# Moving a layer's weight-sum transfers in the schedule, and adding the residual by accumulating stores

## The chip, the core and the metric

The kernel runs on one core of a Trainium2 chip. The metric is the device time of one execution in microseconds (us). TensorE (PE in the profile) multiplies, VectorE (DVE) and ScalarE (ACT) do elementwise work, GpSimd (POOL) does some elementwise work and issues a few transfers, and SyncE (SP) issues nearly all transfers.

## What is computed

One decoder layer on 512 tokens of width 2048, all in float32. Cut to what matters here:

```
h = rms_norm(x, norm_w) * (1 + scale) + shift        # scale, shift, gate from silu(c) @ w_ada
proj = h @ w_in                                      # 2048 x 21056
y_a = (sliding-window attention * silu gate) @ w_o_swa
y_b = (gated delta rule over 16 key / 32 value heads, normed, gated) @ w_o_dn
y = sigmoid(mg_a) * y_a + sigmoid(mg_b) * y_b
return x + gate * (y @ w_out)
```

## The kernel before

**Products.** Every projection is made from tiles of 128 output channels by 512 tokens. `channel_tile` (L244) loops over 16 blocks of 128 input channels, and `mm3` (L237) makes each block's product of three 128x512 matmuls (L240 to L242), because each float32 operand is kept as a high and a low part in a matmul format. So one tile is 48 matmuls. Its weights are one transfer of 1 MB on SP's queue (`load_job`, L200, tile `raw`), and each half of it (24 matmuls) is split into `whi` by a cast on ACT (L52) and `wlo` by a subtraction on DVE (L53). There are two `raw` buffers and three of each split half. A half that is not split in time stops PE.

**Stages.** A startup makes h while `w_ada` (32 MB) streams in. The key stretch follows: 31 tiles (12 key heads, 16 merge gates of one branch, 3 of the other), and beside them the generators of 16 key heads (`keys`, L679) with their convolution (`conv`, L572), transposes, decay matrices `E` and stores, and a triangular solve on DVE (`solve`, L767) in two halves. Then 16 rounds of `heads` (L816), each with five tiles (q, v, v, z, z) and a generator `queries` (L846) and `scan` (L926) that carries the delta rule; then branch B, attention, and `finish` (L1299), where the output product runs on seven products in place of eight and so needs sums of blocks of `w_out`.

**What sets the order.** `channel_tile` calls `pump` (L81) after every second block, eight times a tile, and each call moves the live generators on. A scheduler then puts all instructions in order, each engine's in a fixed one, by its own estimate of when each can start; each engine runs its list in order and waits where an operand is missing. `behind` (L105) adds an order without a semaphore: what is made inside stands after the last matmul so far. Instructions without it may be put earlier in the lists, as early as their data allow.

**The weight sums.** `weight_sums` (L657) makes 16 sums of 1 MB in DRAM (tiles `wsm`): for each a plain copy from DRAM to DRAM on SP's queue (L671), then a transfer on POOL's queue that adds a second block to it (L675). Some copies read an earlier sum, so SP waits at them until that accumulating transfer has landed. `heads` registers this generator as a side queue at 0.15 steps a pump (L643), without `behind`. `finish` reads the sums as `raww` (L1371).

**The output.** `columns` (L1401) multiplies a 128x512 result by the gate on DVE (L1404), loads the matching piece of x on SP's queue (L1406), adds it on POOL (L1407) and stores the sum on SP's queue (L1408), 16 times.

Of the kernel before, what the change touches and what calls it, by code (L numbers as in the profile page):

```python
# [7 lines left out]
F32 = mybir.dt.float32  # L8
# [3 lines left out]
ALU = mybir.AluOpType  # L12
# [4 lines left out]
P = 128  # L17
T = 512
D = 2048
KT = D // P  # L20
NTB = T // P
# [15 lines left out]
class Layer:  # L37
# [552 lines left out]
    def deltanet(self):  # L590
        tc, nc, a = self.tc, self.nc, self.a
        dram = self.dram
        self.lt_d = dram.tile([2, 2, 16, 4, HD, HD], F32, name="lt_d")
        self.lab_d = dram.tile([VH, HD, 4, HD], F32, name="lab_d")
        self.ta_d = dram.tile([2, 16, 4, HD, HD], F32, name="ta_d")
        self.ts_d = dram.tile([2, 2, 16, 4, HD, HD], F32, name="ts_d")
        self.kT_d = dram.tile([KH, P, T], F32, name="kT_d")
        self.k_d = dram.tile([KH, P, T], F32, name="k_d")
        self.o_d = dram.tile([VH, P, T], F32, name="o_d")
        self.ws_d = {k: dram.tile([P, 2048], F32, name=f"ws{k[0]}{k[1]}{k[2]}") for k in self.sum_keys()}  # L600
        with ExitStack() as ps:
            self.pmm = ps.enter_context(tc.tile_pool(name="pmm", bufs=2, space=PSUM, reuse_waits="tile"))
            self.ptp = ps.enter_context(tc.tile_pool(name="ptp", bufs=2, space=PSUM, reuse_waits="tile"))
            self.gwk = ps.enter_context(tc.tile_pool(name="gwk", bufs=1, reuse_waits="tile"))
            sol1 = ps.enter_context(tc.tile_pool(name="sol1", bufs=1, side="right", reuse_waits="tile"))
            with ExitStack() as sa:
                wk = sa.enter_context(tc.tile_pool(name="dnA", bufs=2, reuse_waits="tile"))
                sol0 = sa.enter_context(tc.tile_pool(name="sol0", bufs=1, reuse_waits="tile"))
                gp = sa.enter_context(tc.tile_pool(name="gates", bufs=1, reuse_waits="tile"))
                self.go(self.gates(gp), 1)  # L610
                self.keys_done, self.solve_in = [], {}
                self.keep_order = True
                for g in range(NST):
                    self.go(self.keys(wk, g, self.acc_k[g]), 10 + 8 * g)
                for j in range(NFIRST):
                    self.merge_gate("mb", j, self.mb_d)
                self.go(self.solve_load(sol0, 0), 1)
                self.go(self.solve_load(sol1, 1), 1)
                s0 = self.paced(self.solve(sol0, 0, nc.vector), 0.82)
                s1 = self.paced(self.solve(sol1, 1, nc.vector), 0.0)  # L620
                for kind, j in self.mixed():
                    if kind == "k":
                        self.go(self.keys(wk, j, self.channel_tile(f"k{j}")), 0)
                    else:
                        self.merge_gate("mb", j, self.mb_d)
                        if j == KT - 3:
                            s0[1] = 1.2
                for j in range(3):
                    self.merge_gate("ma", j, self.ma_d)
                    if s0 not in self.slow:  # L630
                        s1[1] = 1.1
                self.drain_live()
                self.drain_slow(s0)
                self.keep_order = False
                s1[1] = 0.6
            with ExitStack() as sb:
                wk = sb.enter_context(tc.tile_pool(name="dnB", bufs=2, reuse_waits="tile"))
                self.tt = []
                for n in range(4):
                    t = wk.tile([P, NTB, P], F32, tag=f"tt{n}", name=f"tt{n}", bufs=1)  # L640
                    nc.gpsimd.memset(t[HD:P, :, 0:HD], 0.0)
                    self.tt.append(t)
                self.beside(self.weight_sums(), 0.15, "ws")  # L643
                for g in range(KH):
                    if g == 8:
                        self.drain_slow(s1)
                    self.heads(wk, g)
                for j in range(3, 5):
                    self.merge_gate("ma", j, self.ma_d)
                self.drain_live()  # L650
                self.drain("ws")
        self.dump("o", self.o_d)

    def sum_keys(self):
        return [(s, n, i) for s in ("m7", "m5", "m6", "m4") for n in range(2) for i in range(2)]

    def weight_sums(self):  # L657

        nc = self.nc
        for n in range(2):  # L660
            for i in range(2):
                w = lambda c, r: self.a["w_out"][2 * c + n, 2 * r + i]
                m7, m5, m6, m4 = (self.ws_d[s, n, i] for s in ("m7", "m5", "m6", "m4"))
                steps = [
                    [(m7, w(1, 0), w(1, 1)), (m5, w(0, 0), w(1, 0))],
                    [(m6, m7, w(0, 0))],
                    [(m4, m6, w(0, 1))],
                ]
                for parts in steps:
                    for dst, src, _ in parts:  # L670
                        nc.sync.dma_start(out=dst, in_=src)  # L671
                    for _ in range(2):
                        yield
                    for dst, _, more in parts:
                        nc.gpsimd.dma_start(out=dst, in_=more, accum_op=ALU.add, max_dma_last_dim=8192)  # L675
                    for _ in range(2):
                        yield
# [697 lines left out]
    def output(self, es, wk, A):  # L1375

        tc, nc, a = self.tc, self.nc, self.a
# [23 lines left out]
        def columns(n, c, t, src, sign):  # L1401

            csl = slice(c * 1024 + n * T, c * 1024 + n * T + T)
            nc.vector.scalar_tensor_tensor(out=src, in0=src, scalar=sign, in1=gt[:, c, :], op0=ALU.mult, op1=ALU.mult)  # L1404
            x = wk.tile([P, T], F32, tag="yb", name="x")
            nc.sync.dma_start(out=x, in_=a["x"][t * P : (t + 1) * P, csl])  # L1406
            nc.gpsimd.tensor_tensor(out=src, in0=src, in1=x, op=ALU.add)  # L1407
            nc.sync.dma_start(out=self.out[t * P : (t + 1) * P, csl], in_=src)  # L1408

        def evict(n, name):  # L1410
            TT = nc.vector.tensor_tensor
            for t in range(2):
                b = ps[name, t]
                if name == "m1":
                    o = t * 1024 + n * T
                    nc.sync.dma_start(out=gt[:, t, :], in_=self.gate_d[o : o + T].partition_broadcast(P))
                if name in ("m1", "m5"):
                    k = wk.tile([P, T], F32, tag=f"{name}{t}", name=name, bufs=1)
                    nc.scalar.copy(out=k, in_=b)
                    keep[name, t] = k  # L1420
                elif name == "m2":
                    c = wk.tile([P, T], F32, tag="m", name="c11")
                    TT(out=c, in0=b, in1=keep["m1", t], op=ALU.add)
                    columns(n, 0, t, c, 1.0)
                elif name == "m6":
                    u1, u5 = keep["m1", t], keep["m5", t]
                    u = wk.tile([P, T], F32, tag="m", name="u2")
                    TT(out=u, in0=b, in1=u1, op=ALU.add)
                    TT(out=u1, in0=ps["m7", t], in1=u, op=ALU.add)
                    c = wk.tile([P, T], F32, tag="m", name="c22")  # L1430
                    TT(out=c, in0=u1, in1=u5, op=ALU.add)
                    TT(out=u5, in0=u, in1=u5, op=ALU.add)
                    columns(n, 1, 2 + t, c, 1.0)
                elif name == "m4":
                    k = keep["m1", t]
                    TT(out=k, in0=b, in1=k, op=ALU.subtract)
                    columns(n, 0, 2 + t, k, 1.0)
                elif name == "m3":
                    k = keep["m5", t]
                    TT(out=k, in0=b, in1=k, op=ALU.add)  # L1440
                    columns(n, 1, t, k, -1.0)
# [3 lines left out]
        for i, (n, m, p) in enumerate(items):  # L1445
            name, s, _ = order[m]
# [128 lines left out]
```

## Time and profile before

| what | value |
|---|---|
| runs | 2982.72, 2983.65, 2976.06 us; median 2982.72 |
| profiled execution | 2981.72 us, span 2980.0 us |
| PE busy over the span | 2887.5 us (97%) |
| DVE, ACT, POOL busy | 59%, 36%, 8% |
| moved by the transfer queues | 497.26 MB, mean 167 GB/s |
| of it on POOL's queue (software_dynamic) | 16.78 MB in 2304 packets |
| landing of a 1 MB accumulating transfer | 8.7 / 12.4 / 16.0 us (min, median, max) |

The span is the time from the first to the last recorded instruction; 1.72 us of the profiled execution lie outside it. A busy PE counts overlapping matmuls once. The granted clock is the share of TensorE's full clock in a stretch. A wait is put down to what arrived last.

### The profile page before, as it was taken

Reading aid. Unit: us, or ns where it says so; the run is one execution under the profiler, and the core shown is the slowest. Engines: PE = TensorE matmul, PEld = TensorE weight load, DVE = VectorE, ACT = ScalarE, POOL = GpSimd, SP = SyncE. Lnnn points to the kernel's source line nnn. Section 1 sums busy time; section 2 is a strip of 40 time slices with the busy share of each in tenths; the row PEclk is TensorE's granted clock in tenths of the full one; section 3 lists DMA queues with packets and bytes.
Section 4 is the critical chain, followed back from the end, with each engine's and each line's share of the span. In section 5 each row is a group of like instructions: output and inputs, shape, how many; then the busy total and the mean of one; then the engine's idle time right before and its main releaser. Section 6 shows DMA issues by size and latency. Waiting matters only on the chain. (4 is left out here: it accounts for less than half of the span.)

```text
span 2980.0 us, 38116 instructions
## 1 busy us (share of the span) xinstructions
PE 2887.5 (97%) x14556; PEld 2362.6 (79%) x14556; DVE 1743.3 (59%) x2883; ACT 1087.4 (36%) x2113; POOL 240.3 (8%) x220
## 2 busy tenths in 40 slices
PE   8878989999999999999999999999999999999989
PEld 6666777888888888888888878888788788788867
DVE  7745769777777544455555453433656656554485
ACT  4334423333333433333333322311244344342343
POOL 0013112011100100000100000000100000000012
PEclk9998999999999999999999999999999999999999
DMA  9898695643333533334332475554322222375575
GB/s 387 308 277 245 201 260 167 196 149 122 112 124 122 150 121 107 125 113 133 115 125 95 168 284 203 185 172 163 110 87 87 77 100 101 109 255 172 180 263 204
DMA packets 179592, 497.26 MB, mean 167 GB/s; under 512 B 73137, under 2 KB 75697, under 8 KB 139601
## 3 DMA queue, kind: packets, MB, share of 16 engines
q1 hardware_dynamic: 177106, 478.06, 47.3%
q0 software_dynamic: 2304, 16.78, 2.9%
q8 instruction: 114, 1.87, 0.3%
q14 instruction: 68, 0.56, 0.1%
HBM read 433.09 MB, written 93.00 MB: 177 GB/s over the span
## 5 line engine op out<-in xcount | busy, mean ns | idle before, releaser
L240 PE MATMUL mm<-hh,whi 128*128 128x512 f32 x2784 | 1137.3, 409 | 9.9 <-ACT whi L52 9.2
L242 PE MATMUL mm<-hh,wlo 128*128 128x512 f32 x2784 | 1094.6, 393 | 0.6 <-DVE wlo L53 0.5
L241 PE MATMUL mm<-hl,whi 128*128 128x512 f32 x2784 | 1091.9, 392 | 0.0
L53 DVE TENSOR_TENSOR wlo<-raw,whi 128x1024 fp32r<-128x1024 f32 (+1 forms) x428 | 523.8, 1227 | 522.6 <-ACT whi L52 518.3
L52 ACT CAST whi<-raw 128x1024 fp32r<-128x1024 f32 (+1 forms) x428 | 445.1, 1043 | 940.7 <-PE mm L241 904.0
L240 PEld LDWEIGHTS mm<-hh,whi 128*128 128x128 f32 x2784 | 527.2, 189 | 120.9 <-ACT whi L52 10.3
L242 PEld LDWEIGHTS mm<-hh,wlo 128*128 128x128 f32 x2784 | 525.7, 189 | 116.9 <-DVE wlo L53 2.5
L241 PEld LDWEIGHTS mm<-hl,whi 128*128 128x128 f32 x2784 | 527.5, 189 | 99.9 <-issue 0.8
L240 PE MATMUL mm<-oh,whi 128*128 128x512 f32 x512 | 200.3, 393 | 1.1 <-ACT whi L52 0.9
L242 PE MATMUL mm<-oh,wlo 128*128 128x512 f32 x512 | 199.4, 390 | 0.5 <-DVE wlo L53 0.5
L241 PE MATMUL mm<-ol,whi 128*128 128x512 f32 x512 | 199.5, 390 | 0.0
L893 POOL TENSOR_TENSOR qe<-qe,yq 128x512 f32<-128x512 f32 x32 | 50.5, 1596 | 902.3 <-DMA qe<-eg_rows 850.7
L240 PEld LDWEIGHTS mm<-oh,whi 128*128 128x128 f32 x512 | 96.1, 188 | 22.9 <-ACT whi L52 1.3
L241 PEld LDWEIGHTS mm<-ol,whi 128*128 128x128 f32 x512 | 96.1, 188 | 21.4 <-issue 1.0
L242 PEld LDWEIGHTS mm<-oh,wlo 128*128 128x128 f32 x512 | 96.1, 188 | 21.1 <-DVE wlo L53 1.2
L792 DVE TENSOR_TENSOR A<-A,atmp 128x62 f32<-128x62 f32 (+30 forms) x124 | 111.0, 895 | 1.5
L785 DVE TENSOR_TENSOR atmp<-A 128x62 f32<-128x62 f32 (+30 forms) x124 | 109.0, 879 | 1.4
L742 POOL TENSOR_TENSOR E<-E,neg_g 128x512 f32<-128x512 f32 x64 | 75.4, 1183 | 260.2 <-DMA E<-g_rows 146.5
L53 DVE TENSOR_TENSOR wlo<-raww,whi 128x1024 fp32r<-128x1024 f32 x56 | 70.8, 1268 | 26.2 <-ACT whi L52 24.7
L52 ACT CAST whi<-raww 128x1024 fp32r<-128x1024 f32 x56 | 58.8, 1052 | 59.7 <-PE m L242 46.1
L939 DVE SCALAR_TENSOR_TENSOR r<-pp,neg_eg,vt 128x128 f32<-128x128 f32 x96 | 29.2, 346 | 78.8 <-PE pp L936 77.6
L1260 ACT ACTIVATE sm<-sm,mx,rs 128x256 f32<-128x256 f32 (+1 forms) x128 | 71.7, 561 | 3.3 <-DVE mx L1255 3.3
(326 smaller groups left out, 3154.2 us busy)
## 6 DMA issues: line engine op xcount, KB each, us to landing
raw<-in_w_ch SPq DMA_DIRECT2D x158, 1024.0 KB
wa<-in_w_ada_ss SPq DMA_DIRECT2D x32, 1024.0 KB
raw<-in_w_od SPq DMA_DIRECT2D x32, 1024.0 KB
wsm<-in_w_out POOLq DMA_DIRECT2D x16, 1024.0 KB, 12.4
E<-g_rows SPq DMA_DIRECT2D x64, 256.0 KB
gw<-in_w_ada_gate SPq DMA_DIRECT2D x16, 1024.0 KB
raw<-in_w_os SPq DMA_DIRECT2D x16, 1024.0 KB
raww<-wsm SPq DMA_DIRECT2D x16, 1024.0 KB
```

The source lines that it names most:

```text
L52: self.nc.scalar.copy(out=hi, in_=src)
L53: self.nc.vector.tensor_tensor(out=lo, in0=src, in1=hi.bitcast(F32), op=ALU.subtract)
L240: nc.tensor.matmul(ps, lhsT=wh, rhs=xh, start=first, stop=False)
L241: nc.tensor.matmul(ps, lhsT=wh, rhs=xl, start=False, stop=False)
L242: self.last_mm = nc.tensor.matmul(ps, lhsT=wl, rhs=xh, start=False, stop=last).ins
L742: nc.gpsimd.tensor_tensor(out=E, in0=E, in1=ng, op=ALU.add)
L785: eng.tensor_tensor(out=t, in0=A[:, m : m + 1, m + 1 :].to_broadcast([P, m, n]), in1=A[:, :m, m : m + 1].to_broadcast([P, m, n]), op=ALU.mult,
L792: eng.tensor_tensor(out=A[:, :m, m + 1 :], in0=A[:, :m, m + 1 :], in1=t, op=ALU.add)
L893: nc.gpsimd.tensor_tensor(out=qf, in0=qf, in1=q, op=ALU.mult)
L939: nc.vector.scalar_tensor_tensor(out=r[:, e, :], in0=pp[:, e, :], scalar=self.neg_eg[:, c, 2 * g + e : 2 * g + e + 1], in1=v[e][:, c, :], ...
L1260: nc.scalar.activation(t, t, AF.Exp, scale=r[:, h : h + 1], bias=mx[:, h : h + 1], accum_out=den[:, h : h + 1])
```

## The change

The generator of the weight sums is wrapped so that each of its steps is made inside `behind`. It first copies x into the output, four transfers of 1 MB. `columns` no longer loads x, adds it and stores, but lets POOL's queue add the gated result to the output in DRAM.

```
-                self.beside(self.weight_sums(), 0.15, "ws")
+                self.beside(self.ordered(self.weight_sums()), 0.15, "ws")
...
+    def ordered(self, gen):
+
+        for _ in range(1000):
+            with self.behind():
+                if next(gen, self) is self:
+                    return
+            yield
+
     def weight_sums(self):
 
         nc = self.nc
+        for t in range(NTB):
+            s = slice(t * P, (t + 1) * P)
+            nc.sync.dma_start(out=self.out[s], in_=self.a["x"][s])
+            yield
...
-            x = wk.tile([P, T], F32, tag="yb", name="x")
-            nc.sync.dma_start(out=x, in_=a["x"][t * P : (t + 1) * P, csl])
-            nc.gpsimd.tensor_tensor(out=src, in0=src, in1=x, op=ALU.add)
-            nc.sync.dma_start(out=self.out[t * P : (t + 1) * P, csl], in_=src)
+            nc.gpsimd.dma_start(out=self.out[t * P : (t + 1) * P, csl], in_=src, accum_op=ALU.add)
```

In the lists of the changed kernel the same line of code stands 12 lines further on (9 in `columns`). Three places show how the lists move.

SP's queue at the start of the key stretch, before: `mb_d` is a merge gate's store, `g_rows` and `eg_rows` are the decay rows that the key heads read, `wsm` are the weight sums.

```order
L671 DMA wsm_1142<-in_w_out 16x16384
L266 DMA mb_d<-mth 128x512
L671 DMA wsm_1153<-wsm_1149 16x16384
L568 DMA g_rows<-rows 32x512
L568 DMA eg_rows<-rows 32x512
L200 DMA raw<-in_w_ch 128x2048
```

The same place in the changed kernel:

```order
L266 DMA mb_d<-mth 128x512
L568 DMA g_rows<-rows 32x512
L568 DMA eg_rows<-rows 32x512
L568 DMA b_rows<-rows 32x512
L200 DMA raw<-in_w_ch 128x2048
```

All 32 transfers of the sums have left the key stretch on SP and on POOL. The four copies of x stand among the first round's loads of `heads`, and the sums are spread over the rounds behind it.

ACT's list in the first round of `heads`, before: `yv` and `th` belong to the convolution of a value tile, `zh` and `zth` to a gate tile, `whi` are the split weights that PE waits for.

```order
L576 ACTIVATE yv<-mm,convh 128x512
L730 ACTIVATE junk,ss<-ptq 128x128
L52 CAST whi<-raw 128x1024
L730 ACTIVATE junk,ss<-ptq 128x128
L887 ACTIVATE E<-E 128x512
L730 ACTIVATE junk,ss<-ptq 128x128
L585 ACTIVATE th<-yv 128x512
L52 CAST whi<-raw 128x1024
L843 COPY vt<-ptv 128x512
L52 CAST whi<-raw 128x1024
L576 ACTIVATE yv<-mm,convh 128x512
```

The same place in the changed kernel:

```order
L576 ACTIVATE yv<-mm,convh 128x512
L742 ACTIVATE junk,ss<-ptq 128x128 x2
L585 ACTIVATE th<-yv 128x512
L855 COPY vt<-ptv 128x512
L576 ACTIVATE yv<-mm,convh 128x512
L585 ACTIVATE th<-yv 128x512
L52 CAST whi<-raw 128x1024 x2
L899 ACTIVATE E<-E 128x512 x2
L840 ACTIVATE zh<-mm,dnwh 128x512
L842 ACTIVATE zth<-mm 128x512
L52 CAST whi<-raw 128x1024 x2
```

Of the three casts that stood between the two `yv` none is left there: two follow the second `yv` and its `th`, and the next two follow `zh` and `zth`, which read the gate tile that PE has then finished.

DVE's list at the end of the first round's scan, before: `S`, `r` belong to the scan, `yq` to the next round's query convolution, `A` and `atmp` to the second triangular solve, `ms` begins the output norm.

```order
L976 SCALAR_TENSOR_TENSOR S<-S,egl,pd 128x128 x2
L53 TENSOR_TENSOR wlo<-raw,whi 128x1024
L580 SCALAR_TENSOR_TENSOR yq<-mm,convh,yq 128x511
L792 TENSOR_TENSOR A<-A,atmp 128x17x46
L580 SCALAR_TENSOR_TENSOR yq<-mm,convh,yq 128x510
L939 SCALAR_TENSOR_TENSOR r<-pp,neg_eg,vt 128x128 x2
L580 SCALAR_TENSOR_TENSOR yq<-mm,convh,yq 128x509
L587 SCALAR_TENSOR_TENSOR yq<-th,yq 128x512
L785 TENSOR_TENSOR atmp<-A 128x810
L53 TENSOR_TENSOR wlo<-raw,whi 128x1024
L792 TENSOR_TENSOR A<-A,atmp 128x18x45
L989 SCALAR_TENSOR_TENSOR ms<-osq,epsq 128x4 x2
```

The changed kernel has there no split at all:

```order
L988 SCALAR_TENSOR_TENSOR S<-S,egl,pd 128x128 x2
L580 SCALAR_TENSOR_TENSOR yq<-mm,convh,yq 128x511
L951 SCALAR_TENSOR_TENSOR r<-pp,neg_eg,vt 128x128 x2
L580 SCALAR_TENSOR_TENSOR yq<-mm,convh,yq 128x510
L580 SCALAR_TENSOR_TENSOR yq<-mm,convh,yq 128x509
L587 SCALAR_TENSOR_TENSOR yq<-th,yq 128x512
L1001 SCALAR_TENSOR_TENSOR ms<-osq,epsq 128x4 x2
```

and after ten small rows of the reciprocal root (L59 to L64) it goes on with the norm (`osb`), the gating of the transposed output (`zh`) and only then the splits:

```order
L873 TENSOR_SCALAR epsq<-ss 128x4
L1008 TENSOR_TENSOR osb<-osb,roy 128x512 x2
L1015 TENSOR_TENSOR zh<-pto,zh 128x512 x2
L53 TENSOR_TENSOR wlo<-raw,whi 128x1024 x2
L804 TENSOR_TENSOR A<-A,atmp 128x17x46
```

PE's list of the changed kernel at that place, where `pp`, `pv`, `po` are the scan's last chunk, `ptq` the next round's query transposes and `pto` the output transposes:

```order
L977 MATMUL po<-vn,E 128x128
L948 MATMUL pp<-S,kT 128x256
L958 MATMUL pv<-r,tt_4601 128x128
L976 MATMUL po<-S,qe 128x128
L958 MATMUL pv<-r,tt_4603 128x128
L977 MATMUL po<-vn,E 128x128
L976 MATMUL po<-S,qe 128x128
L977 MATMUL po<-vn,E 128x128
L274 MATMUL ptq<-ident,yq 128x128 x4
L274 MATMUL pto<-ident,osb 128x128 x8
```

Before, the same rows had twelve products of the next tiles between `pp` and `pv`, between `pv` and `po`, and more ahead of `pto`; now they follow each other with none between. From the second round on the order on PE is as before.

## The prediction

> **What bounds the kernel now.** I read the slices of the page first. PE is busy nearly everywhere but at the start and the very end.
>
> ```profile
> PE   8878989999999999999999999999999999999989
> PEclk9998999999999999999999999999999999999999
> DMA  9898695643333533334332475554322222375575
> ```
>
> One slice is 74.5 us. The seven first ones hold the holes, and there the transfer engines are most loaded. Next come busy times by stage; the columns are length, PE busy, PE's weight loads, DVE, ACT, POOL, granted clock, transfer share and GB/s.
>
> ```profile
> 125.00:475.00 350.00, 300.85 (x1337) 242.91 (x1337) 212.96 (x385) 133.95 (x308) 64.97 (x71) 0.92 0.81 241
> 275.00:375.00 100.00, 95.50 (x443) 77.74 (x442) 68.27 (x134) 39.69 (x92) 16.66 (x18) 0.98 0.67 210
> 700.00:1700.00 1000.00, 998.22 (x5252) 830.35 (x5251) 566.54 (x1015) 377.72 (x832) 87.58 (x80) 1.00 0.38 121
> 2850.00:2910.00 60.00, 52.27 (x215) 40.20 (x214) 48.92 (x72) 26.58 (x37) 8.31 (x6) 0.97 0.79 267
> ```
>
> In the key stretch (125 to 475 us) PE idles 350 - 300.85 = 49.2 us, and runs at 0.92 of its clock, which is another 300.85 x 0.08 = 24 us: 73 us in all, or 1.5 us for each idle us. In 275 to 375, where few sums are in flight, it loses 4.5 + 95.5 x 0.02 = 6.4 us in 100. In `heads` it idles 1.8 us in 1000, with the transfer engines 38% busy. So `heads` is bound by PE alone, and the key stretch by something that the sums share. The waits say what; each row has the us in all, the times and the longest.
>
> ```profile
> PE ptkT L274 <- ACT k L696: 13.4, 2, 8.9
> PE mm L240 <- ACT whi L52: 9.2, 3, 6.3
> PE ptk L274 <- DVE rkt L63: 7.6, 1, 7.6
> PE pg L543 <- DVE gy L536: 4.0, 1, 4.0
> PE v L240 <- ACT hh L433: 3.8, 2, 3.3
> DVE rows L567 <- DMA g_rows<-rows: 11.5, 1, 11.5
> DVE gy L522 <- DMA dtb<-in_dt_bias: 4.1, 1, 4.1
> ```
>
> The last two are DVE's own waits there: it stood 11.5 us behind a store. SP's and POOL's lists show why (start, duration, queue).
>
> ```profile
> 157.67 0.81 POOL L675 DMA_DIRECT2D wsm<-in_w_out  x1 [5.34 <-DMA wsm<-wsm]
> 160.35 0.33 SPq L266 DMA_DIRECT2D mb_d<-mth  x1
> 173.68 0.48 SPq L671 DMA_DIRECT2D wsm<-wsm  x1
> 174.25 0.53 SPq L568 DMA_DIRECT2D g_rows<-rows  x1
> ```
>
> SP stands from 160.7 to 173.7 at a copy that reads the sum which POOL issued at 157.67, and behind it wait the `g_rows` store and the next weight load. The sums therefore hurt the key stretch twice, as traffic and as a closed gate on SP's queue.
>
> **The change part by part.** The sum is made against the profiled execution, 2981.7 us; the median lies 1.0 above it.
>
> *The key stretch without the sums.* The upper end: the whole stretch goes at the pace of 275 to 375. Its work is 350 - 73 = 277 us at full clock; at 6.4 lost for 93.6 done it takes 277 + 19 = 296 us, so 54 are won. The lower end: only the waits tied to the sums by name go, 7.6 (SP's gate), 4.0 (the `dtb` load) and 6.3 (the weights at 442 us), 17.9 x 1.5 = 27. The wait for `hh` (3.8) belongs to the startup and stays. What is late next is DVE: its 213 us of work in some 305 us are 70%, as in 275 to 375 (68%), where PE kept its pace. I take 44, nearer the upper end, since that pace is a row of this very stretch.
>
> *The first round of `heads`.* The lists moved there, and lists are kept to. The durations, grouped over the first two rounds (count | busy, mean ns | idle before):
>
> ```profile
> L580 DVE SCALAR_TENSOR_TENSOR yv<-mm,convh,yv 128x511 f32<-128x511 f32 (+2 forms) x18 | 13.4, 743 | 0.2
> L576 ACT ACTIVATE yv<-mm,convh 128x512 f32<-128x512 f32 x6 | 4.1, 684 | 0.1
> L585 ACT ACTIVATE th<-yv 128x512 f32<-128x512 f32 x6 | 3.8, 626 | 7.6 <-DVE yv L580 7.6
> L52 ACT CAST whi<-raw 128x1024 fp32r<-128x1024 f32 x28 | 29.3, 1046 | 44.2 <-PE mm L241 44.2
> L53 DVE TENSOR_TENSOR wlo<-raw,whi 128x1024 fp32r<-128x1024 f32 x28 | 35.8, 1280 | 12.2 <-ACT whi L52 12.1
> L828 ACT ACTIVATE zh<-mm,dnwh 128x512 f32<-128x512 f32 x4 | 2.8, 689 | 0.0
> L830 ACT ACTIVATE zth<-mm 128x512 f32<-128x512 f32 x4 | 2.4, 594 | 0.0
> L939 DVE SCALAR_TENSOR_TENSOR r<-pp,neg_eg,vt 128x128 f32<-128x128 f32 x12 | 3.7, 346 | 5.9 <-PE pp L936 5.9
> L969 ACT ACTIVATE junk<-po 128x128 f32<-128x128 f32 x16 | 4.5, 281 | 0.3
> L996 DVE TENSOR_TENSOR osb<-osb,roy 128x512 f32<-128x512 f32 x4 | 2.6, 688 | 0.1
> 667.39 0.17 DVE L989 SCALAR_TENSOR_TENSOR ms<-osq,epsq 128x4 f32<-128x4 f32 x1 [0.23 <-ACT junk L969]
> 670.41 1.29 DVE L996 TENSOR_TENSOR osb<-osb,roy 128x512 f32<-128x512 f32 x2
> ```
>
> (a) When the second value tile ends, no half of the next tile is split: ACT's `yv` 0.68, three DVE rows 2.23, `th` 0.63, the cast 1.05, then `wlo` 1.28 less the 0.45 us of products that need only `whi`: 5.4 us. (b) At the end of the first gate tile: `zh` 0.69, `zth` 0.59, cast 1.05, `wlo` less 0.45: 3.2. (c) At the end of the second, PE's `pp` waits for DVE's `zh` behind `zth`, and `r` and the split follow: about 5 us with 2.2 us of PE's own work in it, 3. (d) At the end of the scan the chain stands open: `yq` 0.68, one convolution row 0.74, `r` 0.69, `pv`, `vn`, `po` 1.4, two further convolution rows beside them and `th` (some 0.5 beyond), the copy and squares 1.3, the norm 2.3 (from `ms` to `osb`, 667.39 to 670.41, less a solver row of 1.0 us, and `ms` itself), `osb` 1.38, the transposes 0.6, `zh` 1.36, `wlo` 1.28: 12.2 us, with PE's own 4.9 in it and less than a us of slack between: 8. Together 20 idle us, and with the clock 20 x 1.5 = 30 lost. Bounds: 12 (only (a) and (d), at full clock, each hidden by a us or so) and 45 (half as much again for semaphores and the solver's rows on DVE).
>
> *The sums in later rounds.* 16 copies and 16 accumulating transfers over about eight rounds. Their POOL rows take 0.8 us each and POOL is 9% busy there; PE's order is as before. Nothing for traffic that 38% loaded engines take at one end, and at the other the price of the slower rival below; I take 2, near the low end, since 1 MB weight loads stand ahead of the rounds' small loads on the same queue before, too, and PE idles 1.8 us in 1000. The four copies of x go among them.
>
> The Trainium skill ("DMA: Bandwidth & Descriptors", on queues, rings and completion order) speaks against this change: the descriptors of one issuing engine's queue are taken in ring order, so that a load behind a copy waits for it. By that alone the sum would be 30 higher, as in the slower rival. No row before shows a round's load behind a copy, and the rows of `heads` show no harm from the weight loads.
>
> *The finish.* 16 loads of x, 16 POOL additions and 16 stores leave SP's queue, where weight loads stood behind them. In 2850 to 2910 PE loses 7.7 us and 1.6 of clock; DVE is 82% busy there and stays so, so 9 is the upper end. The lower end is -9: the two buffers that `columns` shares with the loads of y come free only when the accumulating transfer has landed, which for 1 MB takes 8.7 us or more against 4 for addition and store. I take 3 won.
>
> *The tail.* Now the last gate products are followed by additions and stores:
>
> ```profile
> 2973.29 1.28 DVE L1404 SCALAR_TENSOR_TENSOR m<-m,gt 128x512 f32<-128x512 f32 x2
> 2974.05 2.86 POOL L1407 TENSOR_TENSOR m<-m,x 128x512 f32<-128x512 f32 x2 [4.72 <-DVE m L1404]
> 2975.72 1.56 SPq L1408 DMA_DIRECT2D out<-m  x2
> DMA to landing us min/median/max: 8.7/12.4/16.0
> ```
>
> The last store is out at 2977.3 and the span ends at 2980.0, 2.7 us on. With two issues of 0.8 us from 2974.0 the second starts at 2974.8; landing 2.7 us after its issue's end gives 2978.3, 8.7 after its start 2983.5. From -1.7 to +3.5, I take +1, since a quarter of a megabyte is nearer the small one.
>
> **Sum:** -44 + 30 + 2 - 3 + 1 = -14, so 2967.7 for the profiled execution and **2969** for the median.
>
> **The rivals.**
>
> *The key stretch stays bound by its own chains* (only the named waits go, 27): -27 + 30 + 2 - 3 + 1 = +3, 2986. For it: most of the idle us end at ACT or DVE, not at a transfer. Against it: 275 to 375 has the same chains and loses 6.4%.
>
> *The first round costs little* (12): 2951. For it: before, nothing stood there. Against it: each link is a row in one list, and no engine can pass it.
>
> *Slower: a copy holds up a round's loads.* Copies go on SP's queue ahead of a round's `E` and `qe`, and ACT stands at `E` until POOL has masked it:
>
> ```profile
> 127.74 0.63 SPq L671 DMA_DIRECT2D wsm<-in_w_out  x1
> 135.09 0.99 POOL L675 DMA_DIRECT2D wsm<-in_w_out  x1 [134.64 <-DMA wsm<-in_w_out]
> ACT E L887 <- POOL E L743: 73.2, 26, 5.7
> ```
>
> A copy took about 7 us. ACT stands 2.8 us a time at `E` and up to 5.7, and PE does not notice. With a copy just ahead, 2.8 + 7 - 5.7 = 4 us reach PE, 6 with the clock; five such rounds are 30 us, in all 2999. It decides from the point where a copy stands less than some 4 us ahead of `E`; in the new list three weight loads and more lie between from the second round on, which speaks against it. It is the ring order of the Trainium skill (same page and section) as a mechanism of this kernel.
>
> *The change does not do what it says:* the lists exclude it, the sums have moved.
>
> **How the numbers follow.** The forecast, 2956 to 2980: 50% (36 of it beyond 0.3%, 14 within). The first round cheap or more won, below 2956: 18%, all faster. The chains stay, 2980 to 2993: 20%, 16 within 0.3% and 4 slower. The copies in the way, above 2993: 12%, slower. 0.3%, 9 us, is about what a measurement of this kernel can tell from no change. So faster 0.54, same 0.30, slower 0.16. The range 2943 to 2993 leaves out the 12% above and about 5% below.
>
> **What would show it.** Right: SP's rows at 160 us without a gap of 13 us; idle plus clock loss between 125 us and the first query tile down from 73 to about 30 us; waits of PE for `whi` of some 5, 3, 3 us and one of 8 us or more at transposes and split, all within 50 us of the first round; PE busy as before from the second round on. Wrong: no such waits, or the key stretch with its old holes, or ACT waiting for `E` longer than 5.7 us in later rounds.

## The result, and the profile after

The changed kernel takes 2952.57 us (median of 6 runs, 2949.87 to 2959.09), the kernel before 2981.71 beside it. The ratio is 0.9905, 95% interval 0.9887 to 0.9923: 0.95% faster, 29 us, about twice the 14 that were forecast. The profiled execution took 2957.62 us with a span of 2955.9, 24.1 less than before's span; it is one of the slower of the six, 5 us above their median, so the stage sums below come to 24 and not to 29.

The slices of the page (one is 73.9 us): the holes in the first slices are gone but for the startup, and the transfers are spread.

```profile
PE   8899999899999999999999999999999999999988
PEclk9999999999999999999999999999999999999999
DMA  9747555656565854333332575554322232274575
```

Busy times by stage (length, PE, weight loads, DVE, ACT, POOL, clock, transfer share, GB/s). The second row is the first round of `heads`, which now starts at 537:

```profile
125.00:475.00 350.00, 339.60 (x1602) 277.37 (x1601) 271.93 (x454) 153.78 (x351) 68.44 (x61) 1.00 0.55 171
537.00:660.00 123.00, 108.18 (x524) 85.68 (x523) 79.96 (x126) 36.53 (x80) 18.01 (x17) 0.93 0.60 190
700.00:1700.00 1000.00, 996.01 (x5221) 826.58 (x5220) 560.94 (x998) 377.22 (x821) 97.60 (x93) 1.00 0.49 154
```

Between 125 and 475 us PE idles 10.4 us in place of 49.2, at full clock in place of 0.92, and gets 265 more matmuls done. In the first round PE idles 14.8 us and loses 108.18 x 0.07 = 7.6 by the clock; before, this round had no hole. PE's waits between 125 and 475 (us in all, times, longest) are those of the startup and crumbs:

```profile
PE v L240 <- ACT hh L433: 3.8, 2, 3.3
PE ptkT L274 <- ACT k L708: 3.1, 4, 1.2
PE mm L240 <- ACT whi L52: 1.6, 2, 1.3
```

SP's rows at the place where it stood 13 us at a sum go through without a gap:

```profile
157.47 0.33 SPq L266 DMA_DIRECT2D mb_d<-mth  x1
159.44 0.34 SPq L568 DMA_DIRECT2D g_rows<-rows  x1
161.26 0.31 SPq L568 DMA_DIRECT2D eg_rows<-rows  x1
163.29 0.30 SPq L568 DMA_DIRECT2D b_rows<-rows  x1
164.42 0.35 SPq L200 DMA_DIRECT2D raw<-in_w_ch  x1
```

The first round's holes are rows of PE (start, duration; in brackets the idle time before, and who ended it):

```profile
563.71 0.79 PE L240 MATMUL mm<-hh,whi 128*128 128x512 f32 x1 [4.79 <-ACT whi L52]
581.06 0.50 PE L240 MATMUL mm<-hh,whi 128*128 128x512 f32 x1 [2.20 <-ACT whi L52]
598.48 0.70 PE L948 MATMUL pp<-S,kT 128*128 128x256 f32 x2 [1.45 <-DVE S L985]
624.13 1.78 PE L274 MATMUL pto<-ident,osb 128*128 128x128 f32 x8 [2.65 <-DVE osb L1008]
627.83 0.80 PE L242 MATMUL mm<-hh,wlo 128*128 128x512 f32 x1 [1.06 <-DVE wlo L53]
```

ACT's rows ahead of the first of them show the moved list at work: the casts run as soon as `th` is through, and nothing there waits for a transfer. The weight halves had landed, since SP issued no weight load between 543.78 and 566.08 and the transfer engines stood idle from 559 to 561 (share 0.01); their casts stood behind.

```profile
558.97 0.69 ACT L576 ACTIVATE yv<-mm,convh 128x512 f32<-128x512 f32 x1 [0.81 <-PE mm L242]
562.10 0.63 ACT L585 ACTIVATE th<-yv 128x512 f32<-128x512 f32 x1 [2.45 <-DVE yv L580]
562.63 1.98 ACT L52 CAST whi<-raw 128x1024 fp32r<-128x1024 f32 x2
```

To sort the time by stages I take the start of the query convolution's `yq` on ACT as a time mark of each round, first of before (first, third and last round), then of after:

```profile
592.51 0.68 ACT L576 ACTIVATE yq<-mm,convh 128x512 f32<-128x512 f32 x1
723.97 0.68 ACT L576 ACTIVATE yq<-mm,convh 128x512 f32<-128x512 f32 x1
1600.95 0.68 ACT L576 ACTIVATE yq<-mm,convh 128x512 f32<-128x512 f32 x1
```

```profile
536.96 0.68 ACT L576 ACTIVATE yq<-mm,convh 128x512 f32<-128x512 f32 x1
692.63 0.68 ACT L576 ACTIVATE yq<-mm,convh 128x512 f32<-128x512 f32 x1
```

The key stretch ends 55.5 us earlier, and by the third round 31.3 of that are left: the first round gave 24.2 back.

The tail: the last product's row starts at 2945.47 and lasts 0.39, and the span ends at 2955.9, 10.0 us later; before it was 2972.64 to 2980.0, 7.4.

```profile
2946.51 1.28 DVE L1416 SCALAR_TENSOR_TENSOR m<-m,gt 128x512 f32<-128x512 f32 x2
2947.48 1.75 POOL L1417 DMA_DIRECT2D out<-m  x2 [6.67 <-DVE m L1416]
```

### The profile page after: what moved, and what is told of

Same layout as the page of the kernel before. It is cut to its first block, busy times and chain, and to the rows that moved or that the text cites. A ratio compares the mean times of both kernels' runs of the same rounds, so it can differ in the third digit from the quotient of the medians.

```text
span 2955.9 us, 38055 instructions
## 1 busy us (share of the span) xinstructions
PE 2880.3 (97%) x14556; PEld 2354.2 (80%) x14556; DVE 1744.2 (59%) x2883; ACT 1085.7 (37%) x2113; POOL 232.7 (8%) x220
## 4 chain that ended last, share of the span: by engine, by line
PE 71%; issue 16%; DMA 2%; DVE 2%; ACT 1%; POOL 1%; SPq 0%; POOLq 0%; DVEq 0%; ACTq 0%
PE mm L240 21%; PE mm L242 20%; PE mm L241 20%; PE pv L958 1%; PE po L977 1%; PE pp L948 1%; PE po L976 1%; PE S L1248 1%; PE pd L973 1%; DMA oraw<-o_d 1%; DMA qe<-eg_rows 1%; PE pP L274 1%; PE O L1299 1%; PE pqk L909 1%; PE ptv L274 0%
## 5 line engine op out<-in xcount | busy, mean ns | idle before, releaser
L240 PEld LDWEIGHTS mm<-oh,whi 128*128 128x128 f32 x512 | 96.5, 189 | 24.2 <-ACT oh L52 2.0
L52 ACT CAST whi<-raww 128x1024 fp32r<-128x1024 f32 x56 | 58.6, 1051 | 58.3 <-PE m L242 46.8
L580 DVE SCALAR_TENSOR_TENSOR yv<-mm,convh,yv 128x511 f32<-128x511 f32 (+2 forms) x96 | 71.6, 745 | 5.2 <-ACT yv L576 3.5
```

The costliest lines, as they stand in the source:

```text
L52: self.nc.scalar.copy(out=hi, in_=src)
L240: nc.tensor.matmul(ps, lhsT=wh, rhs=xh, start=first, stop=False)
L580: nc.vector.scalar_tensor_tensor(out=y[:, s:], in0=ps[:, : T - s], scalar=w[:, j : j + 1], in1=y[:, s:], op0=ALU.mult, op1=ALU.add)
```

## The experiments

How far each kernel's profiled execution is ahead of before's (us), at the start of the first, third and last round of `heads`, at the end of the last product, and at the end of the span; then the median:

| kernel | 1st round | 3rd | last | products' end | span | median (runs) |
|---|---|---|---|---|---|---|
| changed kernel | 55.5 | 31.3 | 30.8 | 26.8 | 24.1 | 2952.57 (6) |
| tie_only | 55.4 | 48.7 | 48.5 | 49.5 | 49.5 | 2933.66 (4) |
| sums_second_round | 55.0 | 55.2 | 55.1 | 53.0 | 53.1 | 2928.82 (4) |
| sums_second_round_again | 56.8 | 57.0 | 57.0 | 55.2 | 55.2 | 2930.61 (5) |
| second_round_accumulated | 54.8 | 55.0 | 27.3 | 25.8 | 23.3 | 2958.11 (4) |
| x_first_second_round | 55.1 | 35.0 | 19.9 | 18.4 | 15.7 | 2965.49 (4) |
| accumulated_small_x | 52.4 | 52.4 | 52.7 | 50.3 | 47.7 | 2934.37 (4) |
| sums_left_out | 55.5 | 55.7 | 55.8 | 56.0 | 56.1 | 2925.92 (1) |
| sums_tiny | 52.1 | 52.3 | 52.7 | 50.7 | 50.7 | 2931.05 (1) |
| sums_tiny_accumulation | 46.1 | 46.3 | 46.8 | 47.3 | 47.3 | 2934.42 (1) |
| sums_plain_on_pool | 37.9 | 38.0 | 38.3 | 34.4 | 34.4 | 2947.38 (1) |
| sums_early_copies | 18.3 | 18.6 | 19.0 | 14.0 | 14.0 | 2967.82 (1) |
| sums_no_gate | 4.8 | 4.8 | 4.9 | 2.5 | 2.2 | 2979.58 (1) |

The eight kernels with no sum in the key stretch lie between 52.4 and 56.8 at the first mark. One profiled execution of each, against one of before, therefore tells differences of some 4 us from nothing, and no smaller ones.

### Which part of the change does what

**tie_only**: the wrapper of the generator stays, the four copies and the accumulating stores go.

```
-        for t in range(NTB):
-            s = slice(t * P, (t + 1) * P)
-            nc.sync.dma_start(out=self.out[s], in_=self.a["x"][s])
-            yield
...
-            nc.gpsimd.dma_start(out=self.out[t * P : (t + 1) * P, csl], in_=src, accum_op=ALU.add)
+            x = wk.tile([P, T], F32, tag="yb", name="x")
+            nc.sync.dma_start(out=x, in_=a["x"][t * P : (t + 1) * P, csl])
+            nc.gpsimd.tensor_tensor(out=src, in0=src, in1=x, op=ALU.add)
+            nc.sync.dma_start(out=self.out[t * P : (t + 1) * P, csl], in_=src)
```

> Only the tie: the sums' transfers stand behind the heads' products as in the changed kernel, but x is not copied beforehand, and the output is added on POOL and stored by SP as before. ACT's list of the first round keeps its three casts between the two yv, which the copies of x had moved. Theory (the key stretch won 55.6 us, and the 24 us that the first round gave back come from the lists that the copies of x moved): key stretch 54 to 57 us shorter, first round 0 to 8 us longer, no loss in finish and tail, so 2925 to 2937 us. Rival (the first round loses because the sums themselves stand in it): first round 20 us or more longer, as in the changed kernel, so 2943 to 2955.

Measured 2933.66 us, ratio 0.9842 (0.9825 to 0.9858). The key stretch won 55.4, the first round lost 6.7, the rest nothing: the theory holds and the rival falls. The 6.7 are no moved list but a load that came late: one wait of PE for `lab`, one of the scan's small operands.

```profile
569.16 1.08 PE L913 MATMUL py<-ta,lab 64*64 64x64 f32 x14 [3.90 <-DMA lab<-lab_d]
```

```profile
551.67 0.98 POOL L683 DMA_DIRECT2D wsm<-in_w_out  x1
554.00 1.12 POOL L683 DMA_DIRECT2D wsm<-in_w_out  x1
```

```profile
556.83 0.63 SPq L889 DMA_DIRECT2D lab<-lab_d  x1
```

```profile
560.00:580.00 20.00, 16.10 (x86) 12.29 (x86) 14.70 (x21) 4.19 (x7) 4.90 (x3) 0.83 0.82 233
```

POOL issued two accumulating transfers at 552 and 554, SP the load of `lab` at 557, and it landed only at 569. PE idled 3.9 us and ran at 0.83 of its clock in these 20 us, another 2.7. Two things made the load late. By the trace's landing events it took 12.2 us in place of the 2.4 of the same load in sums_second_round, with both accumulating transfers under way; and SP issued it 4.9 us later than there (556.83 against 551.97), with two plain copies of the sums ahead of it on its list (issued from 534.7 on, landed by 547.3). Either alone would have let it land by 564.2, before PE asked for it at 565.3. The Trainium skill ("TensorE: Matmul & The Clock Gate", Part 1) says that the clock falls to half after an idle window of about 3.4 us; a wait of 3.9 us with a drop fits, but a wait need not be that long here: before's wait of 2.64 us that ended at 301.16 came with a drop too (0.83 from 295 to 305). So my slower rival, a round's load held up, did occur, once, and at 6.7 us (I had 6). The copies on SP's own queue had a part in it by way of the later issue; the load itself was lengthened, as far as these rows show, by transfers of another queue.

**sums_second_round**: as tie_only, but the generator is registered one round later.

```
-                self.beside(self.ordered(self.weight_sums()), 0.15, "ws")
                 for g in range(KH):
+                    if g == 1:
+                        self.beside(self.ordered(self.weight_sums()), 0.15, "ws")
```

> The tie alone again, and the sums begin one round of heads later, so that the first round's lists on ACT are word for word as before; output added and stored as before. Theory (lists of the first round): the whole key stretch is kept, 54 to 57 us, and the first round costs at most 2, so 2924 to 2930 us. Rival (a round loses when its key stretch ends early, whatever its lists say, because DVE's triangular solve then lies more in the round): first round 15 us or more longer, 2940 or more.

Measured 2928.82 us, ratio 0.9825 (0.981 to 0.9841). The first round costs nothing. This is the fastest kernel with the layer's result, 24 us faster than the changed one.

**second_round_accumulated**: the same with the changed kernel's output, the four copies of x at the end of the generator.

```
                     for _ in range(2):
                         yield
+        for t in range(NTB):
+            s = slice(t * P, (t + 1) * P)
+            nc.sync.dma_start(out=self.out[s], in_=self.a["x"][s])
+            yield
```

> The tied sums from the second round on, as in the run with the sums in the second round, and the output by accumulating stores, with x copied into the output behind all sums, two rounds before the end of the heads' list of sums. It differs from that run in the output alone. Theory (what the accumulating stores cost in the changed kernel was +2.0 in the finish and +2.7 in the tail): 4 to 6 us slower than 2928.8, 2932 to 2936. Rival (3 won in the finish and 1 lost in the tail, as predicted): 2925 to 2928.

Measured 2958.11 us, ratio 0.9921 (0.9904 to 0.9938): both theories were wrong by 22 us or more. I had priced the stores and overlooked the copies: 27.6 us are lost in the tenth and eleventh round, in which they stand and take effect.

**x_first_second_round**: the four copies ahead of the sums, in the second round.

> The same, but the four copies of x stand ahead of the sums, in the second round, where ACT's list then has two casts behind the second yv and its th, as the changed kernel had them in the first round. Theory (the moved lists cost the time, in whichever round): 15 to 30 us slower than with the copies behind the sums, 2947 to 2966. Rival (only the first round is hurt, since it has no round before it and the second solver beside it): within 6 us of it, 2931 to 2940.

Measured 2965.49 us, ratio 0.9938 (0.9923 to 0.9952). The time itself lies in the theory's range, but the difference to second_round_accumulated is only 7 us, because that kernel too had paid for its copies; both expectations had missed that. By the marks 28.8 us go in the second round and its neighbour (55.1 to 26.3 at the fourth round's), and 6.4 more in the sixth, around a wait of PE of 4.0 us for DVE's `vs` whose cause stays open. The two kernels lose in different rounds, 540 us apart, in the same steps; PE's rows, first of x_first_second_round, then of second_round_accumulated:

```profile
673.77 0.80 PE L240 MATMUL mm<-hh,whi 128*128 128x512 f32 x1 [4.20 <-ACT whi L52]
676.57 0.79 PE L242 MATMUL mm<-hh,wlo 128*128 128x512 f32 x1 [1.58 <-DVE wlo L53]
693.46 0.94 PE L274 MATMUL ptq<-ident,yq 128*128 128x128 f32 x4 [4.57 <-DVE yq L587]
```

```profile
1213.82 0.80 PE L240 MATMUL mm<-hh,whi 128*128 128x512 f32 x1 [4.20 <-ACT whi L52]
1216.63 0.79 PE L242 MATMUL mm<-hh,wlo 128*128 128x512 f32 x1 [1.58 <-DVE wlo L53]
1233.31 1.11 PE L274 MATMUL ptq<-ident,yq 128*128 128x128 f32 x4 [4.58 <-DVE yq L587]
```

Waits that repeat to a hundredth of a us point to an order, not to contention. In the later kernel the copies were issued from 1137.7 to 1164.7, and the holes lie from 1183 to 1239; neither ACT nor DVE waits for any transfer between 1140 and 1245, and the transfer engines are 15% busy where the holes are:

```profile
1183.00:1240.00 57.00, 38.89 (x164) 29.56 (x165) 20.51 (x46) 17.93 (x47) 3.34 (x4) 0.88 0.15 51
```

The lists did move: against sums_second_round, row by row, some 20 of ACT's 56 rows and 118 and 55 of PE's 356 stand elsewhere in these two rounds. ACT's rows ahead of the 4.20 show two pairs of `zh` and `zth` first and the cast behind them.

```profile
1210.60 0.68 ACT L841 ACTIVATE zh<-mm,dnwh 128x512 f32<-128x512 f32 x1
1211.17 0.60 ACT L843 ACTIVATE zth<-mm 128x512 f32<-128x512 f32 x1
1211.65 0.70 ACT L841 ACTIVATE zh<-mm,dnwh 128x512 f32<-128x512 f32 x1
1212.22 0.62 ACT L843 ACTIVATE zth<-mm 128x512 f32<-128x512 f32 x1
1212.70 2.02 ACT L52 CAST whi<-raw 128x1024 fp32r<-128x1024 f32 x2
```

**accumulated_small_x**: as second_round_accumulated, with x in pieces.

```
-        for t in range(NTB):
-            s = slice(t * P, (t + 1) * P)
+        for t in range(16):
+            s = slice(t * 32, (t + 1) * 32)
```

> The kernel with the sums from the second round on, and the output by accumulating stores; x is copied into the output in 16 pieces of 256 KB in place of four of 1 MB, behind the sums, so that PE's list stays word for word that of the kernel with the sums in the second round, and ACT's casts stand as there up to the finish. The same 4 MB of x in the same rounds as in the run that lost 27.6 us there. Theory (the moved lists, not the copies' bytes, cost that round): the round loses 0 to 2 us; what is left is the price of the accumulating stores, 4 to 6 us (finish 2.0, tail 2.7): 2932 to 2936. Rival (the bytes of x in a round): 20 us or more are lost in those rounds, 2950 or more.

Measured 2934.37 us, ratio 0.9835 (0.9819 to 0.9851). No round loses anything (52.4 at the third, 52.7 at the last). The pieces were spread over 162 us (1139.9 to 1301.9), so this run changes both the lists (at most 3 of ACT's rows and 4 of PE's stand elsewhere in any round, against sums_second_round) and the pace of the bytes. That it is the lists rests on the rows above: nothing there waits for a transfer, and the transfer engines are mostly idle. The tail is 10.0 us again (products' end 2922.30, span 2932.3).

**sums_second_round_again**: the kernel of that row, unchanged, on the same chip.

> The kernel with the sums from the second round on and the output added and stored as before, once more beside the last one on the same chip: 2926 to 2932 us, 4 to 6 us faster than it by the theory of its row; the predicted finish and tail (3 won, 1 lost) would have it 2 us slower than it.

Measured 2930.61 us, ratio 0.9826 (0.9811 to 0.9841): faster than its neighbour by 3.8, just under the 4 to 6 expected and with intervals that overlap. By the rows the tail is 7.3 us (2917.48 to 2924.8) against 10.0, so the accumulating stores cost 2.7 there. From the last round to the products' end the kernels with accumulating stores lost 4.0, 1.5, 1.5 and 2.4 us against before, those with plain stores lost 1.8 and 2.1 or won 1.0: no price that stands out.

### Why the sums cost so much in the key stretch

**sums_left_out**: the generator isn't registered, and `out_load` takes `w_out[n, i]` for a sum.

> The kernel before with no weight sums at all: no transfer of them anywhere, and the output product reads plain blocks of w_out where it read sums, so that its loads stay the same in number and size (the result is not the layer's). Theory (the sums in the key stretch cost what the changed kernel won there): key stretch 54 to 58 us shorter and nothing else, 2923 to 2929 us. Rival (a part of the gain comes from other lists of the changed kernel, not from the sums' absence): less than 48 us won in the key stretch.

Measured 2925.92 us (one execution, as for all that follow); key stretch 55.5. All that the tie won there is the sums' absence.

**sums_no_gate**: two sources are replaced.

```
-                    [(m6, m7, w(0, 0))],
-                    [(m4, m6, w(0, 1))],
+                    [(m6, w(0, 0), w(0, 0))],
+                    [(m4, w(0, 1), w(0, 1))],
```

> The kernel before, but the eight copies that read an earlier sum read a plain block of w_out in place of it, so that SP no longer stops at them until an accumulating transfer has landed; as many transfers of the same size run in the same stretch (half of the sums' values are other ones, and the result is not the layer's). Theory A (SP's closed gate: 7.6 + 4.0 us of waits behind it, 17 with the clock): 2959 to 2967 us, key stretch 15 to 23 us shorter. Theory B (traffic is what costs, the gate little): 0 to 10 us shorter, 2972 to 2982. Theory C (the gate is nearly all): 45 us or more shorter, below 2937.

Measured 2979.58 us, key stretch 4.8: theory B. SP's closed gate, the one mechanism that I could name from the rows, is a small part. The 4.8 is a balance and hardly above the 4 us that can be told from nothing: by the same products, before's work from 150 to 200 us, where the gate stood, takes 5.9 us less, and that of the next 50 takes 5.2 more, for a reason that the run doesn't show.

**sums_tiny** and **sums_tiny_accumulation**: `dst[0:8]` and `src[0:8]` in all transfers, then in the accumulating ones alone.

> The kernel before, all lists in its own order, but each of the 32 transfers of the sums moves 8 rows of 128, a sixteenth of its bytes, and the output product reads plain blocks of w_out (the result is not the layer's). All waits between the sums' transfers stay, on SP and on POOL; only their bytes go. Theory (traffic): the key stretch is 45 to 56 us shorter, 2925 to 2938 us in all. Rival (SP and POOL standing at the sums' own waits is the cause): less than 25 us shorter, above 2957.

> As the last, but the 16 plain copies keep their full megabyte and only the 16 accumulating transfers are cut to a sixteenth (the result is not the layer's). Theory (traffic, both kinds by their bytes; an accumulating transfer reads two megabytes and writes one, a copy reads one and writes one): 0.6 of the 55 us go, the key stretch 25 to 40 us shorter, 2942 to 2957. Rival (accumulating transfers are what costs, by their small packets): 45 us or more, below 2937. Rival (the copies on SP's queue ahead of the loads are what costs): less than 15 us, above 2967.

Measured 2931.05 and 2934.42 us, key stretch 52.1 and 46.1. The bytes cost 52.1 of the 55.5; the 3.4 left for the bare waits can't be told from nothing. Against my theory of equal bytes the rival holds: the accumulating half is worth 46, the plain half only 6. Its reason, small packets, falls with the next run.

**sums_plain_on_pool**: `accum_op=ALU.add` is taken out, nothing else.

> The kernel before with one thing taken out: the 16 transfers on POOL's queue do not accumulate, they overwrite (a sum is then only its second block, and the result is not the layer's). Queue, size, waits and all lists stay word for word. Cutting these transfers to a sixteenth won 46.1 us up to the first query tile, of the 52.1 that cutting all 32 won. Theory A (accumulation itself is what costs: it holds the transfer engines longer, 78 us of all sixteen for 15.7 MB against 34 for the plain copies): 30 us or more of the 46 are won, 2935 to 2951 us. Theory B (a megabyte on POOL's queue, with POOL and SP waiting for it, costs that much whether it accumulates or not): less than 15 won, above 2967.

Measured 2947.38 us, key stretch 37.9: theory A. Same queue, same bytes, same packets, same lists, and the same transfers to wait for; accumulation alone costs 38 us, of which a part can be longer waits for transfers that land later. The transfer queues between 125 and 475 us (packets, MB, share of 16 engines), first before, then this kernel:

```profile
q1 hardware_dynamic: 35872, 67.29, 56.6%
q0 software_dynamic: 2304, 16.78, 24.4%
```

```profile
q1 hardware_dynamic: 38830, 72.64, 62.4%
q0 software_dynamic: 2304, 16.78, 13.3%
```

For the same 16.78 MB in as many packets the accumulating transfers hold the sixteen engines 350 x 0.244 = 85 us, the plain ones 47. They also land later, 12.4 us (8.7 to 16.0) against

```profile
DMA to landing us min/median/max: 5.8/9.0/11.5
```

**sums_early_copies**: whether it is the held engines or POOL, standing longer at the next sum with the masks of `E` behind it on its list, this run asks. Before, POOL stood at sums for these times (the longest of the first row is the start of the span):

```profile
POOL wsm L675 <- DMA wsm<-in_w_out: 194.8, 6, 134.6
POOL wsm L675 <- DMA wsm<-wsm: 72.4, 8, 21.1
```

Without that first wait they are 133 us.

```
+        for half in range(2):
+            keys = self.sum_keys()[half::2]
+            for k in keys:
+                nc.sync.dma_start(out=self.ws_d[k], in_=w(*pairs[k[0]][0], *k[1:]))
...
+            for k in keys:
+                nc.gpsimd.dma_start(
+                    out=self.ws_d[k], in_=w(*pairs[k[0]][1], *k[1:]), accum_op=ALU.add, max_dma_last_dim=8192
+                )
+                yield
```

> The sums in the key stretch again, all 32 transfers at full size and 16 of them accumulating, but tied to the key stretch's products in two halves: eight copies first, all read from w_out, and behind them eight accumulating transfers, one every seven pumps, so that neither SP nor POOL has to stand at one until an earlier transfer lands (half of the sums have other terms, and the result is not the layer's). Theory A (accumulating transfers cost by holding the transfer engines, so that the key heads' small loads come late): most of the 55 us stay lost, the key stretch is 0 to 18 us shorter than before, 2962 to 2985 us. Theory B (they cost by POOL standing at the next sum while the masks of E wait behind it on POOL's list): 35 us or more are won, below 2950. The lists of the key stretch differ a little from before, which may be worth a few us either way.

Measured 2967.82 us, key stretch 18.3, at the edge of theory A. POOL never stood at a sum in this execution, and 37 of the 55.5 us are lost all the same. They are lost to late transfers: of PE's three longest waits in the stretch, two (10.5 and 7.6 us) end with a cast that had stood for a weight load, and one (7.1) with a copy that had stood for a store of `kT` (8.4). The first of them on PE and on ACT:

```profile
327.12 0.80 PE L240 MATMUL mm<-hh,whi 128*128 128x512 f32 x1 [10.53 <-ACT whi L52]
326.02 1.99 ACT L52 CAST whi<-raw 128x1024 fp32r<-128x1024 f32 x2 [10.21 <-DMA raw<-in_w_ch]
```

So theory A holds with another victim than I had named, SP's 1 MB weight loads and not the key heads' small ones. In all ACT stood 24.3 us for weight loads here and 16.7 before, 2.7 with the plain transfers on POOL's queue, and never in sums_left_out. The transfers alone cost about two thirds of the 55.5; the waits of SP and POOL at them, longer because the transfers land later, at most the other third. The split is rough, since the lists differ and POOL issues two or three sums at once in places. The Trainium skill ("DMA: Bandwidth & Descriptors", Queues, rings and completion order) says that each transfer engine takes turns between the queues that have work for it; that loads on SP's queue come late while POOL's transfers run, as the weight loads did here and `lab` in tie_only, agrees with it.

## Why the prediction was too small by half

The direction of both large terms was right, and two sizes were wrong in the same sense. Of the two mechanisms named for the key stretch the traffic was right, and the closed gate hardly counted (4.8). By the profiled execution:

| term | predicted | measured | by |
|---|---|---|---|
| key stretch | -44 (-27 to -54) | -55.5 | 1st round's mark |
| first round | +30 (12 to 45) | +24.2 | 1st to 3rd mark |
| later rounds | +2 | +0.5 | 3rd to last mark |
| from the heads to the finish | not named | +2.0 | last `yq` to the last `a12h` cast, 2809.53 to 2780.71 |
| finish | -3 (-9 to +9) | +2.0 | `a12h` to products' end |
| tail | +1 (-1.7 to +3.5) | +2.7 | products' end to span |
| sum | -14 | -24.1 | |

The misses partly cancel: the first three terms were 18.8 us too pessimistic, the others 8.7 too optimistic. By luck the total is thus off by 10 and not by 19. The median's 29 holds 5 us more, as said with the result.

- **The key stretch failed, by 11.5.** Two steps of the sum did it. The larger is "I take 44", 10 below the upper end of 54. No row stood behind the 10: the lower end leaned on the waits tied to the sums by name, and sums_no_gate shows how little the gate among them is worth (4.8) and sums_tiny how much the bytes are (52.1); and DVE, named as what is late next, held nothing up. The smaller step is the upper end itself, "the whole stretch goes at the pace of 275 to 375", which the measured gain passes by 1.5. Here are those products and the next hundred us of before's work, paired by PE's rows; the first line is before from 375 to 475, the others are the changed kernel at the products of 275 to 375 and of 375 to 475:

```profile
375.19:475.03 99.84, 86.89 (x383) 70.60 (x382) 71.44 (x100) 32.28 (x69) 19.37 (x20) 0.93 0.83 243
```

```profile
241.25:338.17 96.92, 94.11 (x442) 76.74 (x441) 68.38 (x135) 40.08 (x93) 19.75 (x21) 1.00 0.62 192
338.17:419.47 81.30, 81.30 (x383) 67.57 (x382) 74.61 (x101) 31.97 (x69) 16.27 (x13) 1.00 0.55 171
```

The quiet hundred was nearly undisturbed: without the sums the same products still take 96.9 us and PE idles 2.8 in place of 4.5. Its longest wait before, the 2.64 us that ended at 301.16, fell where the transfer engines were 1% busy and no sum was under way. What failed is that it stood for the whole stretch. The products of 375 to 475 have no such waits of their own: without the sums they run with no idle us and at full clock, 81.3 us for 99.8, with DVE 92% busy. My upper end left 19 us lost in the stretch; in the changed kernel the same work, from 125 to 419, leaves 13 (10.4 idle and 283.6 x 0.01 of clock):

```profile
125.00:419.00 294.00, 283.60 (x1340) 230.78 (x1339) 220.30 (x388) 132.43 (x308) 58.50 (x54) 0.99 0.56 173
```

- **The first round was 6 less than predicted, and inside its bounds.** Of my holes (a) 5.4 was 4.79; (b) and (c), 3 each, were 2.20 with 0.53 behind it, and 1.45 with 0.44; (d), 8, was 5.4 in five pieces. The idle us cost 1.5 each as assumed: 14.8 idle and 7.6 of clock are 22.4 of the 24.2. What I had wrong is whose cost it is: I read the moved lists as the tie's effect. They come with the copies of x, wherever these stand (24.2, 28.8 and 27.6 us in three kernels, each spread over two rounds), and the tie alone leaves three of ACT's casts between the two `yv`. Why the scheduler reorders a round for four copies of 1 MB a step apart, and not for 16 pieces of 256 KB, wasn't tried.
- **Later rounds** were as predicted in the changed kernel. A load held up in a round exists, but the tie_only run shows it once, at the start of the sums, and in part behind another queue's transfers.
- **Finish and tail**: no win of 3. The finish lost 2.0; since kernels with plain stores lost up to 2.1 between the last round and the products' end, that isn't shown to be the accumulating stores' price. The tail's +2.7 lies at the upper end of my bounds: the landing after the second issue's start (2948.1 to the end at 2955.9) took 7.8 us, nearer the 8.7 of a megabyte than the 2.7 of a plain store. I chose the wrong neighbour, by size and not by kind.
- The rival "the first round costs little" gave 2951, close to the result for the wrong reason: the round cost twice its 12, and the key stretch paid for it.

## What to carry to other kernels

The pace of a quiet stretch is a yardstick only for work with the same waits: ask which of its waits the suspected transfers cause, and whether the rest of the stretch has the others at all. A term taken inside its bounds needs a row for the distance to the bound, as the bound itself does. An accumulating transfer isn't priced by its bytes: cut it, make it plain, or move it to a stage whose transfer engines are half idle, and look at which of the three pays. When a scheduler orders the lists, ask of each edit by itself what it moves: here a cheap-looking copy cost as much as half the gain, and taking it out, with the plain stores back and the sums a round later, gave 2929 us in place of 2953.

## What the runs showed of the hardware

- Accumulation on POOL's queue held the transfer engines 1.8 times as long as plain transfers of the same bytes and packets (24.4% against 13.3% of sixteen engines over 350 us), and cost this stretch 46 us where the plain ones cost 8 (46.1, and 46.1 less 37.9).
- Accumulating stores of 256 KB landed 4.0 to 12.3 us after their issue (median 5.2), and the time from the last product to the end of the span is 2.5 to 2.7 us longer in the four kernels that have them (10.0 against 7.4 in the changed kernel).
- A load of 64 KB on SP's queue landed 12.2 us after its issue with two accumulating transfers of 1 MB under way on POOL's queue (tie_only), and 2.4 us after it without them (sums_second_round).
